# Two-layer decoder trunk on one core: nine seven-product pairs in the last SwiGLU, shared sums added to x before the last blocks, nine low parts finished by transfers out of DRAM

## The chip, the cores and the metric

One core of a Trainium2 chip runs the whole program. The metric is the device time of one execution in microseconds (us), lower is better. The kernel before took 966.36 us (median of three runs, 966.13 to 967.34).

## The reference

A trunk of two layers over 256 rows of width 1024, batch 1, all in float32. Each layer is: half a SwiGLU step, a token mixer, half a SwiGLU step. Every step normalises x, scales and shifts it by vectors worked out from c, and adds its result to x through a gate vector. What the change touches is the last SwiGLU step of the last layer, the end of the program:

```
h = modulate(rms_norm(x, norm_g[1, 2]), sh3, sc3)
x = x + 0.5 * g3[:, None, :] * swiglu(h, w_gate, w_up, w_down)
swiglu(h, w_gate, w_up, w_down) = (silu(h @ w_gate) * (h @ w_up)) @ w_down
```

with h of 256x1024, w_gate and w_up of 1024x2816 and w_down of 2816x1024. The 2816 inner columns are 22 blocks of 128, called f = 0 to 21 here.

## The kernel before

**Three passes.** A float32 product is made of float32r parts: each operand is split in a high part hi (ScalarE rounds it, line 775) and a low part lo = value - hi (VectorE, line 780), and TensorE runs hi*hi, hi*lo and lo*hi (lines 932 to 934, function mm3). For the gate and up blocks the moving operand holds hi and lo of both row halves side by side, 512 columns, so a weight block takes one 512-column pass with its hi (line 1192) and one 256-column pass with its lo (line 1189). Weights stream from DRAM through three buffers called raw (SyncE issues the loads, line 904); hi and lo have eight buffers each.

**Gate and up.** In the last SwiGLU, f = 0 to 3 come first, then two f at a time: a gate tile and an up tile of 1024x256, each split in two halves of 128x1024. For four of the gate tiles (f = 8, 12, 16, 20) the low part of the second half is not subtracted by VectorE: ScalarE writes -1 times the raw value, rounded to float32r, into lo's buffer (line 777), and an adding transfer issued on GpSimd adds raw, read from its SBUF buffer, to it (line 778). The raw buffer is free again when that transfer has landed.

**Down in pairs.** Two inner blocks k and k+1 of w_down, with both row halves and both halves of the 1024 output columns, are a 2x2 by 2x2 product: eight 128x128x512 products of three passes. `pair_step` makes it of seven, after Strassen and Winograd: VectorE forms four sums of the left side (`left_sums`, lines 1113 to 1116) and four of the weights (`seven`, lines 879 to 883). Three of the products go to the sums of single output quarters (mm tiles), four to shared sums p1, p6, p7, p5 (tr tiles) which `seven_down` later combines. EARLY says how many pairs stand behind which gate and up block: before, two each behind the blocks that end at f = 5, 9, 13 and 17, eight pairs, k = 0 to 15. After each group the shared sums are copied out of PSUM into SBUF tiles named kept (line 1268) or added to them (line 1264). The remaining k = 16 to 21 of w_down run plainly by STEPS "2 4": a step of two k and a closing one of four, the tail.

**The end.** The quarters are named (row half, column half). Before, the combined shared sum of quarter (1,1) is multiplied by the gate and added to x early (`base`, lines 1316 and 1317); for the other three it is added to the quarter's PSUM sum at the end (line 1050), then follow gate product, addition to x and the transfer out (lines 1052 to 1056, function `resid`). Quarter (1,1) is finished last, in two column halves; the second is made with weights already multiplied by the gate (line 1374), so that one addition (line 1384) and a transfer out (line 1385) end the program.

**The order.** Nothing runs in the order of the code. `Order` records all instructions, places them with a table of durations and rules, and fixes each engine's order; TRIALS is a list of random shifts (a time and a seed), found beforehand, that are applied one after the other. Where an engine's order says so, an instruction waits behind the one ahead of it.

Of the kernel before, what the change touches and what calls it, by code (L numbers as in the profile page):

```python
# [12 lines left out]
F32 = mybir.dt.float32  # L13
F32R = mybir.dt.float32r
# [3 lines left out]
ALU = mybir.AluOpType  # L18
AX = mybir.AxisListType
PSUM = bass.MemoryType.PSUM  # L20
DRAM = bass.MemoryType.DRAM

P = 128
# [6 lines left out]
FB = 512  # L30
TAIL = 4
B1 = 7
STEPS = {(1, 0): "4 p p 4 4 2 4", (1, 1): "2 4"}
PAIRED = {(1, 0): 12, (1, 1): 0}
EARLY = {(1, 1): {6: 2, 10: 2, 14: 2, 18: 2}}
SLOTS = 10
DMA_AT = [("gate", f) for f in range(8, 22, 4)]
BEFORE = {key: sum(EARLY.get(key, {}).values()) for key in STEPS}
PAIRS = {key: steps.count("p") + BEFORE[key] for key, steps in STEPS.items()}
BY_DMA = [("ffn_w_" + n, (1, 1), f * P) for n, f in DMA_AT]  # L40
# [174 lines left out]
def bcast_row(ap, n, parts=P):  # L215
# [23 lines left out]
MARGIN = 400.0  # L239
ROUND_OF_ORDER = 2  # L240
PORT = 250.0

TRIALS = ((22.03, 5), (28.53, 74), (28.53, 181), (22.87, 220), (27.57, 328), (27.57, 471), (34.83, 1096),
# [18 lines left out]
ENGINES = ("PE", "DVE", "Activation", "Pool", "SP")  # L262


def elements(ap):
    return math.prod(c for _, c in ap.ap[1:])
# [51 lines left out]
class Order:  # L318
# [4 lines left out]
    def __init__(self, nc, tc, rank, held, late, anchor):  # L323
# [14 lines left out]
        n = len(self.ins)  # L338
# [4 lines left out]
        for ks in sums.values():  # L343
# [3 lines left out]
        self.cost = [duration(i, a) for i, a in zip(self.ins, self.aps)]  # L347
        self.mode = [self.pe_mode(i, a) for i, a in zip(self.ins, self.aps)]
        self.two = [type(i).__name__ in ("InstTensorTensor", "InstCustomDveAnt") for i in self.ins]
        self.table = [{"Silu": "s", "Sin": "s", "Exp": "e"}.get(str(getattr(i, "func", "")).rsplit(".", 1)[-1])  # L350
                      if e == "Activation" else None for i, e in zip(self.ins, self.eng)]
        self.succ, self.after = [[] for _ in range(n)], [[] for _ in range(n)]
# [13 lines left out]
        for name, us in self.uses.items():  # L366
            t = self.tiles[name]
# [98 lines left out]
    def place(self, need, until=1e15):  # L466

        n = len(self.ins)
# [7 lines left out]
        in_pool, pool_end = {}, {}  # L476
        for t, r in self.ring.items():
            in_pool[r[0]] = in_pool.get(r[0], 0) + users[t]
        flight, dma_free, mode, table, idle_from, wide, paired = [], FIRST_BYTE, None, None, 0.0, 0, 0.0

        def grant(r):
# [53 lines left out]
        while placed < n:  # L535
# [36 lines left out]
                occ, dur, mode = occ + d, dur + d, now  # L572
            if e == "DVE" and self.two[k]:
                paired = t + occ
            if e == "Pool" and not self.dma[k]:
                at_once = [x for x in avail["DVE"]] + [(need[j], j) for r, j in known["DVE"] if r < t + PORT]
                lock = paired
                if at_once and free["DVE"] < t + PORT and self.two[min(at_once)[1]]:
                    lock = max(free["DVE"], t) + self.cost[min(at_once)[1]][0]
                d = lock - t - 150.0  # L580
                occ, dur = occ + max(d, 0.0), dur + max(d, 0.0)
# [89 lines left out]
def trunk(ctx: ExitStack, tc: tile.TileContext, a: dict, out: bass.AP):  # L671
    nc = tc.nc
# [96 lines left out]
    c_b = cp.tile([P, D], F32, name="c_b")  # L769


    def split(src, n, by_dma=False):
        hi = splitp.tile([P, n], F32R, tag="hi", name=nm("hi"))
        lo = splitp.tile([P, n], F32R, tag="lo", name=nm("lo"))
        nc.scalar.activation(hi, src, AF.Copy)  # L775
        if by_dma:
            nc.scalar.activation(lo, src, AF.Copy, scale=-1.0)
            nc.gpsimd.dma_start(lo.bitcast(F32), src, accum_op=ALU.add)
            return hi, lo
        nc.vector.tensor_tensor(lo, src, hi.bitcast(F32), op=ALU.subtract)  # L780
        return hi, lo
# [111 lines left out]
    def wload():  # L893
# [7 lines left out]
        else:  # L901
            raw = rawp.tile([P, kt * cols], F32, tag="raw", name=nm("raw"))
        n = P * kt * cols
        nc.sync.dma_start(raw, a["w"][wpos[0]:wpos[0] + n].rearrange("(p f) -> p f", p=P))
        wpos[0] += n
        if whole:
            return [raw[:, j * cols:(j + 1) * cols] for j in range(kt)]
# [4 lines left out]
        pairs = []  # L912
        for k0 in range(0, kt, per):
            n = min(per, kt - k0)
            hi, lo = split(raw[:, k0 * cols:(k0 + n) * cols], n * cols, parts[0] in BY_DMA and k0 >= kt // 2)
            for j in range(n):
                pairs.append((hi[:, j * cols:(j + 1) * cols], lo[:, j * cols:(j + 1) * cols]))
        return pairs
# [354 lines left out]
    def seven_down(strassen, gT, sums, after, ada_to):  # L1273
# [40 lines left out]
        def base(t, half, y):  # L1314
            x = xs[t][:, halves[half]]
            nc.vector.tensor_tensor(y, y, gate[:, halves[half]], op=ALU.mult)
            nc.vector.tensor_tensor(x, x, y, op=ALU.add)
# [14 lines left out]
            plus(v[:, lo], p7, u[:, hi])  # L1332
            plus(v[:, hi], p5, u[:, hi])
        if at == (1, 1):
            base(1, 1, p5)
            rest = {(0, 0): p1, (1, 0): p7, (0, 1): p6}
        else:
            base(0, 0, u[:, lo])
            base(0, 1, v[:, hi])
# [23 lines left out]
        wl = nextw()  # L1363
        for t in range(NT):
            rows([t], 0, first_tail, wl, end - 1)
            resid(t, 0, acc[t, 0], gate, True, plus=rest[t, 0])
        wl = nextw()
        rows([0], 1, first_tail, wl, end - 1)
        resid(0, 1, acc[0, 1], gate, True, plus=rest[0, 1])
        more = tr_tile()[:, :256]  # L1370
        scaled = adap.tile([P, TAIL * 256], F32, tag="adaw", name=nm("scaled"))
        cs = slice(768, 1024)
# [7 lines left out]
            mm3(last[:, :256], *gT[first_tail + j, 1], *[x[:, :256] for x in w], start=j == 0 and not begun, stop=j == TAIL - 1)  # L1380
        for j in range(TAIL):
            mm3(more, *gT[first_tail + j, 1], *[x[:, j * 256:(j + 1) * 256] for x in ends], start=j == 0, stop=j == TAIL - 1)
        resid(1, 1, last, gate, True, done=256)
        nc.vector.tensor_tensor(xs[1][:, cs], more, xs[1][:, cs], op=ALU.add)
        nc.scalar.dma_start(out[0, P:, cs], xs[1][:, cs])
        after(1)
# [725 lines left out]
```

## Time and profile before

| what | value |
|---|---|
| median of three runs | 966.36 us |
| span of the profiled execution, first to last instruction | 964.5 us |
| PE (TensorE) busy | 959.0 us, 99% |
| DVE (VectorE) busy | 893.7 us, 93% |
| ACT (ScalarE) busy | 642.7 us, 67% |
| POOL (GpSimd) busy | 76.5 us, 8% |
| HBM read | 258.53 MB |
| last SwiGLU, first to last product | about 782 to 961 us of the span |

The profiled execution has no separate time of its own beside its span of 964.5 us; what a run counts around the span is the difference to the runs' median, 1.9 us. The profile gives each engine's busy time, the chain of work that ended last, groups of instructions with their mean durations, who waited for whom, and a timeline. PE's busy time counts pipelined passes that overlap, so a busy PE says that it had something in flight, not that it issued at its best rate: a 512-column pass shows 0.39 us, but the next one starts 0.23 us after it.

### The profile page before, as it was taken

The numbers are of one execution on the slowest core, as the hardware profiler recorded it, in microseconds if no ns is written. First come the engines' busy times: TensorE is split into PE (matmuls) and PEld (weight loads), VectorE is DVE, ScalarE is ACT, GpSimd is POOL, SyncE is SP. The second block draws the span as 40 slices with busy tenths as digits, with TensorE's granted clock in tenths as the row PEclk, the third lists the DMA queues.
The fourth block names the chain that finished last, engine by engine and source line by source line (L and its number), as shares of the span: only waits on it lengthen the run. The fifth ranks groups of instructions, "written<-read, shape, count | busy, mean of one in ns | idle before, by whom it ended". The sixth has DMA issues, their size and how long they took to land.

```text
span 964.5 us, 15470 instructions
## 1 busy us (share of the span) xinstructions
PE 959.0 (99%) x5519; PEld 824.4 (85%) x5519; DVE 893.7 (93%) x1627; ACT 642.7 (67%) x1220; POOL 76.5 (8%) x112
## 2 busy tenths in 40 slices
PE   9999999999999999999999999999999999999998
PEld 7998888888888888888888888888889888888887
DVE  7999999798999999999779899899999879999997
ACT  5688665477757965565358656663689887776662
POOL 0002100012231100000000000000143100000000
PEclk9999999999999999999999999999999999999999
DMA  9978998889796799989878989659553354865761
GB/s 349 408 284 266 366 323 309 352 313 354 278 331 214 271 361 337 338 321 321 341 291 314 333 327 340 233 204 329 179 184 120 117 197 175 272 230 199 259 211 73
DMA packets 57692, 265.85 MB, mean 276 GB/s; under 512 B 7536, under 2 KB 9360, under 8 KB 39696
## 3 DMA queue, kind: packets, MB, share of 16 engines
q1 hardware_dynamic: 55584, 259.12, 73.3%
q0 software_dynamic: 1408, 5.24, 2.3%
q8 instruction: 43, 0.70, 0.3%
q10 hardware_dynamic: 624, 0.51, 0.2%
q14 instruction: 33, 0.27, 0.1%
HBM read 258.53 MB, written 4.22 MB: 272 GB/s over the span
## 4 chain that ended last, share of the span: by engine, by line
PE 94%; DMA 2%; DVE 2%; ACT 2%; issue 1%; SPq 0%; ACTq 0%; DVEq 0%
PE tr L1192 16%; PE mm L932 14%; PE mm L934 14%; PE mm L933 14%; PE mm L1192 9%; PE tr L1189 9%; PE mm L1189 5%; PE at L1479 1%; PE at L1413 1%; PE at L1449 1%; PE tr L932 1%; PE tr L933 1%; PE tr L934 1%; PE mm L2061 1%; PE tr L985 1%
## 5 line engine op out<-in xcount | busy, mean ns | idle before, releaser
L775 ACT ACTIVATE hi<-raw 128x1024 fp32r<-128x1024 f32 (+3 forms) x306 | 307.7, 1028 | 126.9 <-PE mm L934 59.1
L780 DVE TENSOR_TENSOR lo<-raw,hi 128x1024 fp32r<-128x1024 f32 (+3 forms) x302 | 351.8, 1191 | 31.4 <-ACT hi L775 25.9
L1192 PE MATMUL tr<-h,hi 128*128 128x512 f32 x688 | 164.6, 390 | 0.0
L1192 PEld LDWEIGHTS tr<-h,hi 128*128 128x128 f32 x688 | 127.5, 188 | 25.3
L793 DVE CUSTOM_DVE_ANT_0 adaw<-adaw,c_b,cols 128x1024 f32<-128x1024 f32 x96 | 121.9, 1282 | 0.7 <-DMA adaw<-in_ada_dram 0.7
L932 PE MATMUL mm<-hi,gh 128*128 128x512 f32 (+1 forms) x292 | 113.8, 390 | 0.0
L933 PE MATMUL mm<-lo,gh 128*128 128x512 f32 (+1 forms) x292 | 113.3, 388 | 0.0
L934 PE MATMUL mm<-hi,gl 128*128 128x512 f32 (+1 forms) x292 | 113.3, 388 | 0.0
L1192 PE MATMUL mm<-h,hi 128*128 128x512 f32 x416 | 98.2, 391 | 0.2 <-DVE u L1089 0.2
L934 PE MATMUL mm<-hi,h 128*128 128x512 f32 (+1 forms) x240 | 93.1, 394 | 0.0
L932 PE MATMUL mm<-hi,h 128*128 128x512 f32 (+1 forms) x240 | 92.8, 396 | 0.1
L933 PE MATMUL mm<-lo,h 128*128 128x512 f32 (+1 forms) x240 | 92.7, 393 | 0.0
L1192 PEld LDWEIGHTS mm<-h,hi 128*128 128x128 f32 x416 | 77.0, 188 | 15.7 <-DVE u L1089 0.4
L1189 PEld LDWEIGHTS tr<-h,lo 128*128 128x128 f32 x688 | 87.0, 191 | 2.6
L1189 PE MATMUL tr<-h,lo 128*128 128x256 f32 x688 | 87.9, 283 | 0.0
L934 PEld LDWEIGHTS mm<-hi,gl 128*128 128x128 f32 x292 | 54.8, 188 | 11.2
L933 PEld LDWEIGHTS mm<-lo,gh 128*128 128x128 f32 x292 | 54.9, 188 | 10.7
L932 PEld LDWEIGHTS mm<-hi,gh 128*128 128x128 f32 x292 | 54.9, 188 | 10.6
L831 DVE CUSTOM_DVE_ANT_0 adaw<-adaw,c_b,g_cols 128x1024 f32<-128x1024 f32 x48 | 61.5, 1291 | 0.0
L972 POOL TENSOR_TENSOR rstd<-ssq,mhalf 128x1 f32<-128x1 f32 x12 | 13.4, 1117 | 527.5 <-DVE ssq L967 485.2
L1189 PE MATMUL mm<-h,lo 128*128 128x256 f32 x416 | 54.4, 284 | 0.1
L1189 PEld LDWEIGHTS mm<-h,lo 128*128 128x128 f32 x416 | 52.7, 191 | 1.6 <-DVE lo L780 0.2
(291 smaller groups left out, 1607.8 us busy)
## 6 DMA issues: line engine op xcount, KB each, us to landing
raw<-in_w_dram SPq DMA_DIRECT2D x140, 1024.0 KB, 5.9
adaw<-in_ada_dram SPq DMA_DIRECT2D x155, 512.0 KB, 5.8
raw<-in_w_dram SPq DMA_DIRECT2D x14, 512.0 KB, 4.3
bias_d<-bt SPq DMA_DIRECT2D x12, 256.0 KB, 4.4
gate<-gate_d SPq DMA_DIRECT2D x6, 512.0 KB, 6.5
bg<-bias_d POOLq DMA_DIRECT2D x4, 768.0 KB, 6.3
adaw<-in_ada_dram SPq DMA_DIRECT2D x10, 256.0 KB, 5.7
raw<-in_w_dram SPq DMA_DIRECT2D x4, 576.0 KB, 5.1
```

Source lines behind the costliest of these rows:

```text
L775: nc.scalar.activation(hi, src, AF.Copy)
L780: nc.vector.tensor_tensor(lo, src, hi.bitcast(F32), op=ALU.subtract)
L793: nc.vector.tensor_tensor_reduce(wt, wt, c_b, 1.0, b, op0=ALU.mult, op1=ALU.add, accum_out=m_cols[:, i, c:c + 1])
L831: nc.vector.tensor_tensor_reduce(wt, wt, c_b, 1.0, g[:, k:k + 1], op0=ALU.mult, op1=ALU.add, accum_out=g[:, k:k + 1])
L932: nc.tensor.matmul(ps, lh, rh, start=start, stop=False)
L933: nc.tensor.matmul(ps, lh, rl, start=False, stop=False)
L934: nc.tensor.matmul(ps, ll, rh, start=False, stop=stop)
L972: nc.gpsimd.tensor_tensor(r, stats[t], mhalf[:, 0:1], op=ALU.pow)
L985: nc.tensor.transpose(kslice(pt, j), kslice(y, j), ident)
L1189: nc.tensor.matmul(ps[f][i][:, S:], w, hs[0], start=False, stop=k == KD - 1)
L1192: nc.tensor.matmul(ps[f][i], w, hs[2], start=k == 0, stop=False)
L1413: nc.tensor.matmul(ps3[:, i, :], qTs(e, t), kTs(e, nk), start=True, stop=True)
```

## The change

STEPS of the last SwiGLU becomes "4" and EARLY puts three pairs instead of two behind the block that ends at f = 17: nine pairs, k = 0 to 17, and only the tail of four k runs plainly. DMA_AT now names nine gate tiles (f = 4, 6, ... 20). The adding transfer reads its addend from the weight array in DRAM, not from the raw buffer. All four quarters of the shared sums are multiplied by the gate and added to x by `base`, and `resid` has no extra addition any more; quarter (1,1) has no plain products ahead of the tail, so its last sum starts there and its `resid` is half as wide. The planner learns a rule: a GpSimd AFFINE_SELECT (function grips) and a VectorE instruction on SBUF hold each other up. TRIALS is a new list, so every engine's order is new from the first microseconds on.

```
 B1 = 7
-STEPS = {(1, 0): "4 p p 4 4 2 4", (1, 1): "2 4"}
+STEPS = {(1, 0): "4 p p 4 4 2 4", (1, 1): "4"}
 PAIRED = {(1, 0): 12, (1, 1): 0}
-EARLY = {(1, 1): {6: 2, 10: 2, 14: 2, 18: 2}}
+EARLY = {(1, 1): {6: 2, 10: 2, 14: 2, 18: 3}}
 SLOTS = 10
-DMA_AT = [("gate", f) for f in range(8, 22, 4)]
+DMA_AT = [("gate", f) for f in range(4, 22, 2)]
...
+GRIP = 50.0, 725.0, 577.0, 160.0
...
-TRIALS = ((22.03, 5), (28.53, 74), (28.53, 181), (22.87, 220), (27.57, 328), (27.57, 471), (34.83, 1096),
+TRIALS = ((28.52, 62196), (27.3, 97909), (34.82, 84045), (34.77, 72623), (34.58, 54429), (39.69, 96378), (39.67,
...
+        self.grips = [type(i).__name__ == "InstTensorScalarAffineSelect" for i in self.ins]
+        self.port = [e == "DVE" and all(x.tensor.space not in (PSUM, DRAM) for x in a) and max(elements(x) for x in a) > 8
+                     for e, a in zip(self.eng, self.aps)]
...
-            if e == "Pool" and not self.dma[k]:
+            if e == "DVE" and self.port[k]:
+                d = max(0.0, gripped[1] - t) if t >= gripped[0] else 0.0
+                occ, dur = occ + d, dur + d
+                porting = t + occ
+            if e == "Pool" and self.grips[k]:
...
+                dur = max(GRIP[1], lock - t + GRIP[2])
+                occ = dur - 70.0
+                gripped = since, t + dur - GRIP[3]
+            elif e == "Pool" and not self.dma[k]:
...
-    def split(src, n, by_dma=False):
+    def split(src, n, again=None):
...
-        if by_dma:
+        if again is not None:
             nc.scalar.activation(lo, src, AF.Copy, scale=-1.0)
-            nc.gpsimd.dma_start(lo.bitcast(F32), src, accum_op=ALU.add)
+            nc.gpsimd.dma_start(lo, again.bitcast(F32R), accum_op=ALU.add)
             return hi, lo
...
-            hi, lo = split(raw[:, k0 * cols:(k0 + n) * cols], n * cols, parts[0] in BY_DMA and k0 >= kt // 2)
+            at = slice(k0 * cols, (k0 + n) * cols)
+            hi, lo = split(raw[:, at], n * cols, place[:, at] if parts[0] in BY_DMA and k0 >= kt // 2 else None)
...
         if at == (1, 1):
-            base(1, 1, p5)
-            rest = {(0, 0): p1, (1, 0): p7, (0, 1): p6}
+            for t, half, y in ((0, 0, p1), (1, 0, p7), (0, 1, p6), (1, 1, p5)):
+                base(t, half, y)
...
-            resid(t, 0, acc[t, 0], gate, True, plus=rest[t, 0])
+            resid(t, 0, acc[t, 0], gate, True)
...
-        resid(1, 1, last, gate, True, done=256)
+        if begun:
+            resid(1, 1, last, gate, True, done=256)
+        else:
+            resid(1, 1, last[:, :256], gate, True, part=slice(0, 256))
```

The kernel after is 22 to 25 lines longer from there on: line 780 becomes 800, 777 becomes 797, 1192 becomes 1214, 932 to 934 become 954 to 956.

**Place one: the first transfers.** ScalarE's rows before, where the first adding transfer is prepared (lo_9394, gate tile f = 8; hi_9389 and hi_9393 are the two high halves of its tile; gh is the high part of a gated block; g_9425 is the gate sum of f = 6, copied out of PSUM):

```order
L775 ACTIVATE hi_9389<-raw_9387 128x1024
L775 ACTIVATE hi_9393<-raw_9387 128x1024
L777 ACTIVATE lo_9394<-raw_9387 128x1024
L947 ACTIVATE gh_9234<-g_9226 128x256
L947 ACTIVATE gh_9262<-g_9254 128x256
L775 ACTIVATE hi_9495<-raw_9493 128x1024
L1088 ACTIVATE g_9425<-tr_9367 128x256
```

ScalarE's rows after, where the transfer of the gate tile f = 6 is prepared (lo_9336); the kept rows copy the first group's shared sums out of PSUM:

```order
L795 ACTIVATE hi_9331<-raw_9329 128x1024
L795 ACTIVATE hi_9335<-raw_9329 128x1024
L795 ACTIVATE hi_9373<-raw_9371 128x1024
L797 ACTIVATE lo_9336<-raw_9329 128x1024
L1290 ACTIVATE kept_9352<-tr_9298 128x512
L1290 ACTIVATE kept_9356<-tr_9300 128x512
L1290 ACTIVATE kept_9358<-tr_9301 128x512
```

TensorE's rows after at the same place, from the end of the first two pairs (mm_9325) to the first use of lo_9336 (tr_9369 and tr_9370 are gate and up sums of f = 6 in the banks that the kept copies free):

```order
L956 MATMUL mm_9325<-hi_9294,gl_9170 128x512
L1214 MATMUL tr_9369<-h_8818,hi_9331 128x512 x4
L1214 MATMUL tr_9369<-h_8818,hi_9335 128x512 x4
L1214 MATMUL tr_9370<-h_8818,hi_9373 128x512 x4
L1214 MATMUL tr_9370<-h_8818,hi_9377 128x512 x4
L1211 MATMUL tr_9369<-h_8818,lo_9332 128x256 x4
L1211 MATMUL tr_9369<-h_8818,lo_9336 128x256 x4
```

The preparation of a transfer now stands ahead of the copies that free the banks, and its low part is used in the block that follows at once.

**Place two: the end of the last group of pairs.** TensorE's rows before, the last products of the eighth pair and the first gate passes of f = 18 (tr_10389):

```order
L932 MATMUL mm_9324<-hi_10325,gh_10169 128x512
L933 MATMUL tr_10331<-lo_10326,sums_10178 128x512
L934 MATMUL tr_10331<-hi_10325,sums_10178 128x512
L934 MATMUL tr_10330<-hi_10319,sums_10178 128x512
L933 MATMUL mm_9324<-lo_10326,gh_10169 128x512
L934 MATMUL mm_9324<-hi_10325,gl_10170 128x512
L1192 MATMUL tr_10389<-h_8818,hi_10356 128x512 x4
```

TensorE's rows after, the ninth pair (sums_10315, the left sums of f = 16 and 17) and the first gate passes of f = 18 (tr_10446):

```order
L954 MATMUL tr_10344<-hi_10379,sums_10315 128x512
L954 MATMUL tr_10342<-hi_10379,sums_10315 128x512
L954 MATMUL mm_9309<-hi_10374,sums_10315 128x512
L955 MATMUL mm_9309<-lo_10375,sums_10315 128x512
L954 MATMUL tr_10343<-hi_10385,sums_10315 128x512
L955 MATMUL mm_9302<-lo_10375,gh_10306 128x512
L956 MATMUL mm_9309<-hi_10374,sums_10315 128x512
L1214 MATMUL tr_10446<-h_8818,hi_10412 128x512 x4
L1214 MATMUL tr_10446<-h_8818,hi_10416 128x512 x2
L955 MATMUL tr_10344<-lo_10380,sums_10315 128x512
L956 MATMUL tr_10344<-hi_10379,sums_10315 128x512
```

The last pair uses inner blocks that were computed just ahead of it, and gate passes of the next block stand between its products.

**Place three: the end.** VectorE's last rows before (kept tiles are the shared sums, ry is a scratch tile, mm_9301, mm_9324 and mm_9308 the sums of quarters (0,0), (1,0) and (0,1), mm_10647 and tr_10718 the two halves of (1,1)):

```order
L1050 TENSOR_TENSOR kept_9350<-mm_9301,kept_9350 128x512
L1052 TENSOR_TENSOR ry_10679<-kept_9350,gate_9904 128x512
L1053 TENSOR_TENSOR x_94<-x_94,ry_10679 128x512
L1050 TENSOR_TENSOR kept_9356<-mm_9324,kept_9356 128x512
L1052 TENSOR_TENSOR ry_10696<-kept_9356,gate_9904 128x512
L1053 TENSOR_TENSOR x_95<-x_95,ry_10696 128x512
L1050 TENSOR_TENSOR kept_9354<-mm_9308,kept_9354 128x512
L1052 TENSOR_TENSOR ry_10713<-kept_9354,gate_9904 128x512
L1053 TENSOR_TENSOR x_94<-x_94,ry_10713 128x512
L1052 TENSOR_TENSOR ry_10749<-mm_10647,gate_9904 128x512
L1053 TENSOR_TENSOR x_95<-x_95,ry_10749 128x512
L1384 TENSOR_TENSOR x_95<-tr_10718,x_95 128x256
```

VectorE's last rows after (mm_9302, mm_9325, mm_9309, mm_10748 and tr_10741 are the same sums):

```order
L1074 TENSOR_TENSOR ry_10705<-mm_9302,gate_9907 128x512
L1338 TENSOR_TENSOR kept_9354<-kept_9354,gate_9907 128x512
L1075 TENSOR_TENSOR x_94<-x_94,ry_10705 128x512
L1339 TENSOR_TENSOR x_95<-x_95,kept_9354 128x512
L1074 TENSOR_TENSOR ry_10721<-mm_9325,gate_9907 128x512
L1075 TENSOR_TENSOR x_95<-x_95,ry_10721 128x512
L1074 TENSOR_TENSOR ry_10737<-mm_9309,gate_9907 128x512
L1075 TENSOR_TENSOR x_94<-x_94,ry_10737 128x512
L1074 TENSOR_TENSOR ry_10773<-mm_10748,gate_9907 128x256
L1075 TENSOR_TENSOR x_95<-x_95,ry_10773 128x256
L1409 TENSOR_TENSOR x_95<-tr_10741,x_95 128x256
```

The three additions of kept are gone from the end; one quarter's `base` stands among the closing rows, the other three stand ahead of the tail's last low parts.

More of the change, by code (lines that the diff above doesn't have):

```diff
@@ L478, in place @@
             in_pool[r[0]] = in_pool.get(r[0], 0) + users[t]
+        gripped, porting = (0.0, 0.0), 0.0
         flight, dma_free, mode, table, idle_from, wide, paired = [], FIRST_BYTE, None, None, 0.0, 0, 0.0
@@ L574, in place @@
                 paired = t + occ
-            if e == "Pool" and not self.dma[k]:
+            if e == "DVE" and self.port[k]:
[3 more added lines that the diff above has]
+            if e == "Pool" and self.grips[k]:
+                soon = [x[:2] for x in avail["DVE"]] + [(need[j], j) for r, j in known["DVE"] if r < t + GRIP[0]]
+                lock = since = max(porting, t)
+                if soon and free["DVE"] < t + GRIP[0] and self.port[min(soon)[1]]:
+                    lock = max(free["DVE"], t) + self.cost[min(soon)[1]][0]
+                    since = lock - 20.0
+                dur = max(GRIP[1], lock - t + GRIP[2])
+                occ = dur - 70.0
+                gripped = since, t + dur - GRIP[3]
+            elif e == "Pool" and not self.dma[k]:
                 at_once = [x for x in avail["DVE"]] + [(need[j], j) for r, j in known["DVE"] if r < t + PORT]
@@ L903, in wload @@
         n = P * kt * cols
-        nc.sync.dma_start(raw, a["w"][wpos[0]:wpos[0] + n].rearrange("(p f) -> p f", p=P))
+        place = a["w"][wpos[0]:wpos[0] + n].rearrange("(p f) -> p f", p=P)
+        nc.sync.dma_start(raw, place)
         wpos[0] += n
@@ L1365, in seven_down @@
             rows([t], 0, first_tail, wl, end - 1)
-            resid(t, 0, acc[t, 0], gate, True, plus=rest[t, 0])
+            resid(t, 0, acc[t, 0], gate, True)
         wl = nextw()
         rows([0], 1, first_tail, wl, end - 1)
-        resid(0, 1, acc[0, 1], gate, True, plus=rest[0, 1])
+        resid(0, 1, acc[0, 1], gate, True)
         more = tr_tile()[:, :256]
```

38 rows, old and new, of the table TRIALS are left out of this document.

## The prediction

> **What bounds the kernel now.** I read the page's busy times and its chain first, then the stretches, then the timeline where TensorE shows a gap.
>
> ```profile
> span 964.5 us, 15470 instructions
> PE 959.0 (99%) x5519; PEld 824.4 (85%) x5519; DVE 893.7 (93%) x1627; ACT 642.7 (67%) x1220; POOL 76.5 (8%) x112
> PE 94%; DMA 2%; DVE 2%; ACT 2%; issue 1%; SPq 0%; ACTq 0%; DVEq 0%
> ```
>
> TensorE is busy all the time and carries 94% of the chain that ended last. So a pass taken away is time gained where it stood, and work on another engine costs only where it makes TensorE wait. The stretches say where waiting is left (columns: stretch, its length, then busy time and count of PE, PEld, DVE, ACT, POOL, granted clock, DMA share, GB/s):
>
> ```profile
> 0.00:40.00 40.00, 38.31 (x266) 33.75 (x267) 31.90 (x63) 24.22 (x50) 2.36 (x24) 1.00 0.99 371
> 40.00:120.00 80.00, 79.61 (x729) 72.18 (x728) 77.04 (x161) 62.12 (x129) 10.91 (x42) 1.00 0.86 317
> ...
> 320.00:680.00 360.00, 360.00 (x1879) 309.15 (x1878) 335.69 (x520) 215.29 (x372) 4.31 (x3) 1.00 0.85 313
> 680.00:800.00 120.00, 119.93 (x718) 103.52 (x717) 109.23 (x287) 103.61 (x259) 28.29 (x24) 1.00 0.43 148
> 800.00:960.00 160.00, 160.00 (x851) 138.39 (x850) 155.03 (x248) 105.08 (x164) 3.50 (x4) 1.00 0.61 211
> ```
>
> TensorE idles 1.7 us in the first 40, 0.4 in the next 80, and nothing in the last 160 us, where the named parts of the change lie. There VectorE is the neighbour to watch: 155 of 160 us. The end, from the timeline:
>
> ```profile
> 960.48 0.69 DVE L1053 TENSOR_TENSOR x<-x,ry 128x512 f32<-128x512 f32 x1
> ...
> 960.87 0.28 PE L934 MATMUL tr<-hi,gl 128*128 128x256 f32 x1
> 961.27 0.42 DVE L1384 TENSOR_TENSOR x<-tr,x 128x256 f32<-128x256 f32 x1
> 961.73 0.35 ACTq L1385 DMA_DIRECT2D out_dram<-x  x1
> ```
>
> The last addition waits for the last pass, not for VectorE, which came free at 961.17. What follows 960.87 is the same in both kernels: 3.6 us.
>
> **The products.** Passes of 512 and of 256 columns follow each other like this, products first (914.31 to 917.26, thirteen steps in all), then a block's sixteen lo passes and the row behind them:
>
> ```profile
> 914.31 0.39 PE L932 MATMUL mm<-hi,sums 128*128 128x512 f32 x1
> ...
> 917.26 0.39 PE L932 MATMUL mm<-hi,gh 128*128 128x512 f32 x1
> ```
>
> ```profile
> 894.07 2.08 PE L1189 MATMUL tr<-h,lo 128*128 128x256 f32 x16
> 895.98 3.82 PE L1192 MATMUL tr<-h,hi 128*128 128x512 f32 x16
> ```
>
> That is 2.95 / 13 = 0.227 us and 1.91 / 16 = 0.119 us. Step "2" was 2 x 2 x 2 = 8 products, 24 passes; the ninth pair has 7 products, 21 passes. Three passes fewer: **-0.68 us**, all of it on the path, since TensorE has no gap in this stretch. Every other pass remains.
>
> **VectorE and ScalarE in the last SwiGLU.** The prices are in the groups of that stretch (mean ns of one behind the comma):
>
> ```profile
> L780 DVE TENSOR_TENSOR lo<-raw,hi 128x1024 fp32r<-128x1024 f32 x48 | 58.1, 1234 | 2.1 <-ACT hi L775 2.0
> L780 DVE TENSOR_TENSOR lo<-t,hi 128x1024 fp32r<-128x1024 f32 x16 | 19.0, 1233 | 0.0
> L831 DVE CUSTOM_DVE_ANT_0 adaw<-adaw,c_b,g_cols 128x1024 f32<-128x1024 f32 x8 | 10.2, 1286 | 0.0
> L879 DVE TENSOR_TENSOR t<-raw 128x1024 f32<-128x1024 f32 x8 | 9.8, 1230 | 0.0
> L882 DVE TENSOR_TENSOR t<-t,raw 128x512 f32<-128x512 f32 x8 | 5.6, 699 | 0.0
> L1113 DVE TENSOR_TENSOR s<-g,g 128x128 f32<-128x128 f32 x6 | 1.8, 298 | 0.0
> L1050 DVE TENSOR_TENSOR kept<-mm,kept 128x512 f32<-128x512 f32 x3 | 2.1, 692 | 1.1 <-PE mm L934 1.1
> L777 ACT ACTIVATE lo<-raw 128x1024 fp32r<-128x1024 f32 x4 | 4.2, 1047 | 0.0
> L947 ACT ACTIVATE sums<-s 128x512 fp32r<-128x512 f32 x8 | 5.0, 622 | 0.0
> ```
>
> VectorE loses five subtractions for the five new transfers (6.2 us), two for step "2" (2.5), and three additions at the end (2.1): 10.8. It gains a pair: t13 1.23, two half rows of t24 1.4, low parts of 512 once (0.7, as L882) and of 1024 three times (3.7), four left sums (1.2) and their low part (0.7): 8.9; and three more `base`, six rows of 0.69: 4.1. Net +2.2 us on 155 of 160, so it fits, with little over. ScalarE gets about five copies of 1.05 and some of the pair's, 7 to 8 us on 105 of 160: covered. The cover of both is TensorE's gate and up passes, 22 us for two blocks.
>
> The tight spot is the ninth pair, whose left sums come from f = 16 and 17, the blocks just ahead of it. Between the last pass of f = 17 and the first product with sums_10315 stand 40 passes, 9.1 us. In that time VectorE's order has three subtractions or sums of 1.23, three rows of 0.70, two of 256 columns (0.42 as L1384) and four of 0.30 up to the last left sum: 7.8 us; ScalarE's high part (0.62) makes 8.4. It is on time by 0.7 us; the low parts behind it (2.4 us of VectorE) are needed 0.7 to 3.4 us later. If VectorE is on time as before, the cost is 0; if each row takes its full duration with no overlap, about 1 us. I take **+0.2 us**.
>
> **The end.** From the last pass of quarter (0,0) to the last pass of all stand 17 of 512 and 21 of 256 columns: 3.9 + 2.5 = 6.4 us. VectorE has eight rows of 0.69 and two of 0.42 in it: 6.4 us by durations, less as they overlap (0.1 us was free before). Bounds 0 to +0.3; I take **0**. Before, quarter (1,1) had rows of 512 there; they are half as wide now.
>
> **The transfers.** The page of issues gives sizes and the median from issue to landing; then comes the first transfer on GpSimd, with VectorE beside it:
>
> ```profile
> raw<-in_w_dram SPq DMA_DIRECT2D x14, 512.0 KB, 4.3
> raw<-in_first_dram SPq DMA_DIRECT2D x4, 512.0 KB, 9.3
> lo<-raw POOLq DMA_DIRECT2D x4, 512.0 KB, 5.5
> ```
>
> ```profile
> 828.84 1.29 DVE L831 CUSTOM_DVE_ANT_0 adaw<-adaw,c_b,g_cols 128x1024 f32<-128x1024 f32 x1
> 829.23 0.96 POOL L778 DMA_DIRECT2D lo<-raw  x1 [39.91 <-ACT gh L947]
> ```
>
> VectorE's row beside GpSimd's issue keeps its 1.29 us (mean 1.286), so five more issues cost it nothing. No adding transfer out of DRAM is in the trace: the plain load of that size lands in 4.3 us, in the crowded first microseconds in 9.3; I take 5.5, the adding one. GpSimd and its queue have nothing else to do in this stage. At place one, ScalarE prepares lo_9336 ahead of the kept copies. Sixteen passes of 512 and four of 256 lie between the bank's first use and lo_9336's: 4.1 us; and if ScalarE copies p1 as soon as it is done (18 passes earlier, 4.1 us), there are 8.2 us from preparation to use, against 0.9 + 5.5 = 6.4. So 0 if ScalarE is prompt, up to 6.4 - 4.7 = 1.7 us if it is as late as the order allows (4.1 and the copy of 0.6). TensorE waited for none of the four before; I take 0. What goes is a wait of SyncE for the raw buffers:
>
> ```profile
> SPq L904 <- DMA lo<-raw: 18.1, 3, 6.8
> ```
>
> Loads then start earlier; as TensorE waits for no load in this stretch, that gains nothing.
>
> **The new order.** Everything outside the last SwiGLU does the same work in another order. What can be lost or won there is TensorE's idle time. One gap has a cause that the new planner rule knows:
>
> ```profile
> 84.41 1.05 POOL L1587 TENSOR_SCALAR_AFFINE_SELECT bt<-bt 128x512 f32<-128x512 f32 x1 [4.98 <-ACT bt L1585]
> ...
> 84.80 1.73 DVE L831 CUSTOM_DVE_ANT_0 adaw<-adaw,c_b,g_cols 128x1024 f32<-128x1024 f32 x1
> ...
> 88.69 0.36 PE L1189 MATMUL mm<-h,lo 128*128 128x256 f32 x1
> ...
> 89.26 0.96 PE L1192 MATMUL mm<-h,hi 128*128 128x512 f32 x3 [0.21 <-DVE u L1089]
> ```
>
> VectorE's row beside AFFINE_SELECT took 1.73 instead of 1.29 us, the rows behind it came late, and TensorE's next pass began 0.57 us after a 256-column pass instead of 0.12: 0.45 us lost. [...] A planner that knows it can put other work there. Bounds: 1.1 us gained (the 2.1 of the first 120 us less about 1.0 before the first pass), or as much lost by a worse order, for nothing in the order alone says that a wait is gone. I take **-0.5 us**, the row's 0.45.
>
> Sum: -0.68 + 0.2 + 0 + 0 - 0.5 = -1.0 us; span 964.5 becomes 963.5. The median is 1.9 above the span: 966.36 - 1.0 = **965.4 us**.
>
> **The rivals.** *The order pays more.* All 1.1 us of early idle go and the ninth pair costs nothing, and small gaps before 800 us close up too, like this one at the stage's first products:
>
> ```profile
> 781.53 0.82 PE L985 MATMUL tr<-ident,y 128*128 128x128 f32 x6
> 782.42 0.50 PE L932 MATMUL mm<-hi,h 128*128 128x512 f32 x1
> 782.76 0.39 PE L933 MATMUL mm<-lo,h 128*128 128x512 f32 x1
> ```
>
> The transposes end at 782.35, the product starts 0.07 later and its successor 0.34 after it instead of 0.227: 0.2 us. Three such make -0.68 - 1.1 - 0.6 = -2.4, 964.0 us. For it: every engine's order is new, and the rule on AFFINE_SELECT is right. Against: the old order had been searched too. 0.30.
>
> *The gain is eaten at the ninth pair.* VectorE's rows run at full durations, TensorE waits 1 us there, and the new order gives nothing: -0.68 + 1.0 = +0.3, 966.7 us. For: the 0.7 us above is all the room. Against: no wait at all in this stretch before. 0.08.
>
> *The transfers out of DRAM come late (slower).* A landing of 9.3 instead of 5.5 makes 10.2 from preparation, against 8.2 at lo_9336: 2.0 us there, and about 0.5 at each of the eight others, whose low parts also stand behind a few passes of their own block: +6.0 - 1.0 = +5.0, 971.4 us. It decides from a landing of 7.3 us on if ScalarE is prompt. Against: DMA was 0.99 busy where 9.3 was seen, 0.61 here. [...] 0.07.
>
> **How the numbers follow.** The forecast has 0.55, and its own range is 964.2 to 966.4 by the bounds above. The range takes in the better part of the first rival and leaves out the third: 963.4 to 967.0. Faster or slower counts from 0.2%, 1.9 us, about what a measurement of this kernel can tell from no change: faster 0.33 (the first rival and 0.03 of the forecast's low end), slower 0.07, same 0.60.
>
> **What would show it.** Right: PE x5516 against x5519; no PE wait for lo at line 1211; the last addition 0.4 us behind the last pass; AFFINE_SELECT without a gap in PE behind it. Wrong: PE waiting for a landing or for sums in the last SwiGLU, landings of 8 us and more, or a change of PE's time before 780 us of over 1.5 us.

## The result, and the profile after it

The changed kernel takes 974.64 us (median of 6 runs, 974.12 to 980.64) beside 966.39 for the kernel before (6 runs, 966.13 to 968.41): ratio 1.0094, 95% interval 1.0081 to 1.0108. It is 8.25 us slower, where 1.0 us faster was forecast, and lies beyond the range given. Busy times and chain of the changed kernel (TensorE has the 5516 passes forecast, but DMA now holds 6% of the chain):

```profile
span 973.0 us, 15478 instructions
PE 962.4 (99%) x5516; PEld 823.6 (85%) x5516; DVE 895.7 (92%) x1635; ACT 646.0 (66%) x1228; POOL 75.8 (8%) x117
PE 87%; DMA 6%; issue 3%; DVE 2%; ACT 2%; POOL 0%; SPq 0%; ACTq 0%; POOLq 0%; DVEq 0%
```

The page's share of PE is 99% in both and hides the loss. The stretches of the changed kernel show where it is (the columns are those of the prediction):

```profile
40.00:120.00 80.00, 80.00 (x736) 73.02 (x735) 74.76 (x160) 63.83 (x128) 11.67 (x42) 1.00 0.83 308
...
800.00:960.00 160.00, 154.97 (x806) 131.93 (x805) 149.14 (x244) 110.11 (x173) 7.79 (x9) 0.99 0.68 224
```

TensorE idles 5.0 us in the last 160, where it idled nothing before. Milestones say the same: the first product of the last SwiGLU begins at 782.85 us (782.42 before) and the last pass at 969.32 (960.87), so 186.47 - 178.45 = 8.0 us are lost in the last SwiGLU. The 0.4 us ahead of it say little: with the kernel before's own order this product begins at 784.52 in before_dram, below. The two largest of TensorE's waits in the whole program (total, number, longest), and the transfers that it waits for (issues: count, size, median landing):

```profile
PE tr L1211 <- DMA lo<-in_w_dram: 5.0, 4, 3.2
PE tr L1977 <- DVE zeros L1935: 1.0, 1, 1.0
```

```profile
lo<-in_w_dram POOLq DMA_DIRECT2D x9, 512.0 KB, 9.2
```

The landings are 8.0 to 10.5 us, the median 9.2 instead of the 5.5 that was taken. The third of the four waits for lo is the longest; this is TensorE's timeline around it, and the stretches around the fall of the granted clock:

```profile
897.78 0.28 PE L1211 MATMUL tr<-h,lo 128*128 128x256 f32 x1
901.30 2.08 PE L1211 MATMUL tr<-h,lo 128*128 128x256 f32 x12 [3.25 <-DMA lo<-in_w_dram]
903.18 2.76 PE L1214 MATMUL tr<-h,hi 128*128 128x512 f32 x6
```

```profile
898.96:902.38 3.42, 1.08 (x9) 1.08 (x10) 0.25 (x2) 0.24 (x1) 0.00 (x0) 1.00 1.02 386
902.38:905.79 3.41, 3.41 (x13) 2.83 (x12) 2.98 (x8) 2.52 (x5) 0.00 (x0) 0.50 1.03 299
905.79:909.20 3.41, 3.41 (x24) 3.15 (x23) 3.41 (x5) 1.59 (x5) 0.00 (x0) 1.00 0.23 43
```

Behind a wait of 3.25 us the clock is 0.50 for 3.41 us, which costs about 3.41 x 0.50 = 1.7 us more. Then it is 1.00 again. In the 3.42 us ahead of the fall TensorE was busy for 1.08.

**Why a landing is late.** SyncE's and GpSimd's issues of the changed kernel around the second transfer, with ScalarE's row that both wait for:

```profile
823.10 1.04 ACT L797 ACTIVATE lo<-raw 128x1024 fp32r<-128x1024 f32 x1
...
824.17 6.67 SPq L925 DMA_DIRECT2D raw<-in_w_dram  x3
...
824.45 0.86 POOL L798 DMA_DIRECT2D lo<-in_w_dram  x1 [23.14 <-ACT lo L797]
```

ScalarE's copy ends at 824.14. With a DRAM source it is the last reader of the raw buffer, so it lets two things go at once: the next 1 MB load into that buffer, issued 0.03 us later, and the transfer, issued 0.31 us later. What the DMA engines then move, in the 4 us from the transfer's issue (queue, packets, MB, share; q1 are the loads, q0 the transfer) and in the 4 us behind those:

```profile
DMA packets 122, 0.91 MB, mean 228 GB/s; under 512 B 9, under 2 KB 9, under 8 KB 14
...
q1 hardware_dynamic: 121, 0.90, 82.4%
q8 instruction: 1, 0.02, 1.5%
```

```profile
q0 software_dynamic: 144, 0.52, 68.0%
q1 hardware_dynamic: 78, 0.51, 34.8%
```

In the first window there is no packet of the transfer at all; in the second there are all 144. The transfer's packets come behind those of the load that its own buffer has let go; it lands 8.0 us after its issue, and TensorE, which is there sooner, waits:

```profile
832.49 1.70 PE L1211 MATMUL tr<-h,lo 128*128 128x256 f32 x12 [0.86 <-DMA lo<-in_w_dram]
```

### The profile page after: what moved, and what is told of

It reads as the page before. It is cut to its first block, busy times and chain, and to the rows that moved or that the text cites. A ratio compares the mean times of both kernels' runs of the same rounds, so it can differ in the third digit from the quotient of the medians.

```text
span 973.0 us, 15478 instructions
## 1 busy us (share of the span) xinstructions
PE 962.4 (99%) x5516; PEld 823.6 (85%) x5516; DVE 895.7 (92%) x1635; ACT 646.0 (66%) x1228; POOL 75.8 (8%) x117
## 4 chain that ended last, share of the span: by engine, by line
PE 87%; DMA 6%; issue 3%; DVE 2%; ACT 2%; POOL 0%; SPq 0%; ACTq 0%; POOLq 0%; DVEq 0%
PE tr L1214 14%; PE mm L954 12%; PE mm L956 12%; PE mm L955 12%; PE mm L1214 10%; PE tr L1211 8%; PE mm L1211 5%; DMA lo<-in_w_dram 4%; DMA adaw<-in_ada_dram 2%; PE mm L2086 2%; PE at L1504 1%; PE at L1438 1%; PE at L1474 1%; PE tr L2086 1%; PE tr L1606 1%
## 5 line engine op out<-in xcount | busy, mean ns | idle before, releaser
L800 DVE TENSOR_TENSOR lo<-raw,hi 128x1024 fp32r<-128x1024 f32 (+3 forms) x297 | 345.7, 1188 | 27.9 <-ACT hi L795 23.4
L1214 PE MATMUL tr<-h,hi 128*128 128x512 f32 x688 | 168.5, 393 | 0.0
L955 PE MATMUL mm<-lo,gh 128*128 128x512 f32 (+1 forms) x286 | 110.1, 389 | 0.0
L954 PE MATMUL mm<-hi,gh 128*128 128x512 f32 (+1 forms) x286 | 109.9, 389 | 0.0
L956 PE MATMUL mm<-hi,gl 128*128 128x512 f32 (+1 forms) x286 | 109.7, 389 | 0.0
L1211 PE MATMUL tr<-h,lo 128*128 128x256 f32 x688 | 93.3, 284 | 5.0 <-DMA lo<-in_w_dram 5.0
L1211 PEld LDWEIGHTS tr<-h,lo 128*128 128x128 f32 x688 | 89.8, 192 | 9.7 <-DMA lo<-in_w_dram 6.2
L954 PEld LDWEIGHTS mm<-hi,gh 128*128 128x128 f32 x286 | 53.8, 188 | 10.6
```

Source lines behind the costliest of these rows:

```text
L954: nc.tensor.matmul(ps, lh, rh, start=start, stop=False)
L955: nc.tensor.matmul(ps, lh, rl, start=False, stop=False)
L956: nc.tensor.matmul(ps, ll, rh, start=False, stop=stop)
L1211: nc.tensor.matmul(ps[f][i][:, S:], w, hs[0], start=False, stop=k == KD - 1)
L1214: nc.tensor.matmul(ps[f][i], w, hs[2], start=k == 0, stop=False)
```

## The experiments

Twelve kernels ran beside the kernel before, whose median was 966.49 in the first four, then 966.61, 966.64 and 966.58 us. The first four were meant to tell apart the source in DRAM (S), its float32r view (T), nine transfers instead of four (N) and the new order (O).

**sbuf_f32, sbuf_f32r**: the changed kernel's order on every engine, but the transfers read the raw buffer again, as float32 or by float32r names.

```
-nc.gpsimd.dma_start(lo, again.bitcast(F32R), accum_op=ALU.add)
+nc.gpsimd.dma_start(lo.bitcast(F32), src, accum_op=ALU.add)
```

> The changed kernel, every engine's order kept row for row, but the nine adding transfers read their addend from the raw buffer in SBUF with float32 views, as before the change. Theory S (an adding transfer whose source is DRAM lands later) and theory T (the float32r view makes it land later): landings fall from a median of 9.2 to about 5.5 us, TensorE's waits for lo (3.4, 1.0, 0.8 and 0.5 us) go, and with them the stretch of slow passes behind the longest wait (1.5 us): about 974.6 - 7.2 = 967.4 us. Theory N (nine transfers crowd each other, whatever their source): landings stay near 9 us and the time near 974.6. Theory O (the new order is worse by itself): the time stays over 972 with landings at 5.5.

> As the run before it, but source and destination of the transfers are named float32r, as in the changed kernel; the source is the raw buffer in SBUF. Theory S: landings of about 5.5 us and about 967.4 us, as with float32. Theory T: landings of about 9 us and about 974.6 us. Theory N: as theory T here.

Measured: 973.35 us (972.82 to 977.38; ratio 1.0081, 1.0060 to 1.0102) and 972.67 (972.07 to 974.85; 1.0069, 1.0054 to 1.0084). The waits and issues of the first:

```profile
lo<-raw POOLq DMA_DIRECT2D x9, 512.0 KB, 5.4
```

```profile
SPq L929 <- DMA lo<-raw: 71.4, 9, 14.2
```

```profile
PE tr L1218 <- ACT hi L799: 1.1, 1, 1.1
PE tr L958 <- DVE g L1115: 1.0, 2, 0.7
PE tr L959 <- DVE lo L804: 0.9, 2, 0.6
```

```profile
945.98 1.06 ACT L799 ACTIVATE hi<-raw 128x1024 fp32r<-128x1024 f32 x1 [1.53 <-DMA raw<-in_w_dram]
947.09 1.21 PE L1218 MATMUL tr<-h,hi 128*128 128x512 f32 x4 [1.10 <-ACT hi L799]
```

The median landing is short again and TensorE waits for no transfer, yet the time hardly falls. SyncE now waits 71.4 us for buffers that the transfers hold, and TensorE waits in the last SwiGLU for ScalarE's and VectorE's rows. The last two rows show it for the longest of these waits: a load is late, so ScalarE is, and then TensorE; for the others no row here shows it. So T falls: with float32r names the median landing is 5.0 us. S is right on the median landing and wrong on the time: the order was made for buffers that come free early, and TensorE loses on late loads much of what it wins on the transfers. Two of the nine landings are long even so, 9.3 and 9.2 us, with the source in SBUF; load_behind comes back to them.

**before_dram**: the kernel before in its own order, its four transfers read DRAM.

> The kernel before, every engine's order kept, with its four adding transfers reading their addend from DRAM as the changed kernel does. From issue to first use there are 12.9, 9.0, 8.4 and 12.1 us. Theories S and T: landings of about 9 us, so TensorE waits at most about 0.8 us at one or two of the four places: 966.4 to 968 us. Theory N: landings stay at 5.5 and the time at 966.4.

Measured: 966.62 us (965.94 to 968.42; ratio 1.0001, 0.9991 to 1.0010), landings 7.3 in the median instead of 5.5, and no wait of TensorE for them: those four stand 8.4 to 12.9 us ahead of their use. The source alone costs nothing where there is room. The four land in 6.5, 8.0, 5.1 and 8.1 us: the second had a load issued 0.17 us ahead of it, the third none for 3.5 us before and 5.5 us after its issue.

**late_known**: the changed kernel, but the planner takes each transfer to land 3.7 us later; its list of trials is the old one.

> The changed kernel with a planner that knows that these transfers land 3.7 us later; the list of shifts is the same, so the order is new and not searched for. Theory S or T: no wait of TensorE for lo over 0.5 us is left, and the time lies below 974.6 by what the unsearched order does not cost again: 967 to 972 us. Theory O: still 973 or more.

Measured: 976.49 us (976.35 to 978.12; ratio 1.0108, 1.0093 to 1.0123). The waits went elsewhere:

```profile
PE tr L960 <- DVE gl L974: 2.2, 1, 2.2
PE tr L1215 <- DMA lo<-in_w_dram: 1.4, 1, 1.4
```

This run is inconclusive on the transfers, since an order whose trials were found for other delays may be worse by itself. Next to be tested was the reading of the section above, called theory L (in line): a transfer is late because of a load that goes first. S now stands for a read out of DRAM that is late by itself.

**load_behind**: every order as in the changed kernel; behind each transfer GpSimd reads a column of the raw buffer, so that the buffer comes free after the transfer's issue.

```
 nc.gpsimd.dma_start(lo, again.bitcast(F32R), accum_op=ALU.add)
+nc.gpsimd.tensor_tensor(seen, src[:, :1], mhalf[:, 0:1], op=ALU.mult)
```

> The changed kernel with every engine's order as it was; behind each of the nine adding transfers GpSimd reads one column of the raw buffer, so the load that this buffer lets go is issued behind the transfer and not 0.28 us ahead of it. Theory L (in line): a transfer comes late because that load's 1 MB stands ahead of it on the DMA engines, about 3 us. It expects first packets 1.4 to 2.0 us after the issue instead of 4.3 to 4.9, a median landing of 4.5 to 6, no wait of TensorE for lo, and the time less 5.7 (gaps), 1.5 (low clock) and some of 1.7 (smaller waits): 966 to 968. Theory S (a read out of DRAM is late by itself): landings stay at 8 to 9, 973 to 975. Theory O (the new order is worse whatever the transfers do): landings fall, the time stays over 970.

Measured: 968.51 us (967.67 to 970.03; ratio 1.0018, 1.0010 to 1.0027). Issues around the same transfer, the DMA queues in the 4 us from its issue, the landings of all nine, and all of TensorE's waits:

```profile
826.82 0.88 POOL L801 DMA_DIRECT2D lo<-in_w_dram  x1 [22.16 <-ACT lo L800]
...
827.44 0.61 POOL L803 TENSOR_TENSOR seen<-raw,mhalf 128x1 f32<-128x1 f32 x1
...
828.07 6.69 SPq L931 DMA_DIRECT2D raw<-in_w_dram  x3
```

```profile
q0 software_dynamic: 111, 0.45, 64.7%
q1 hardware_dynamic: 16, 0.04, 2.6%
```

```profile
lo<-in_w_dram POOLq DMA_DIRECT2D x9, 512.0 KB, 5.7
```

```profile
PE tr L1983 <- DVE zeros L1941: 1.0, 1, 1.0
PE mm L2092 <- ACT whi L2071: 0.3, 1, 0.3
PE tr L1013 <- ACT y L1008: 0.2, 1, 0.2
```

With the load 1.25 us behind the transfer and not 0.28 ahead, 111 of its 144 packets go in the window that held none, and no wait for lo is left. Of 8.25 us over the kernel before, 1.90 are left; the last SwiGLU takes 179.0 us (785.21 to 964.21) instead of 186.47. L is shown in so far as a load that goes first makes the transfer late: the source is the same and S falls, and there are still nine transfers, so N falls. But for the first, the transfers stand in pairs, 3.6 to 6.3 us apart. The first of each pair and the one that stands alone land in 5.1 to 5.7 us; the second of a pair takes 10.0 to 10.6, behind loads that were issued ahead of it, and has the room. In the changed kernel, all four waits for lo are for the first of a pair.

The two late landings of sbuf_f32 show the other side: a source in SBUF, and late all the same behind two loads that were issued 1.7 and 1.3 us ahead. SyncE's issues and GpSimd's, then the landing:

```profile
830.23 11.98 SPq L929 DMA_DIRECT2D raw<-in_w_dram  x4
...
831.93 0.85 POOL L802 DMA_DIRECT2D lo<-raw  x1 [5.46 <-ACT lo L801]
...
lo<-raw POOLq DMA_DIRECT2D x1, 512.0 KB, 9.3
```

The order of the issues alone does not decide. In the changed kernel one load was issued 0.24 us behind a transfer, and even so the 4 us from the transfer's issue hold packets of the loads alone:

```profile
936.08 0.86 POOL L798 DMA_DIRECT2D lo<-in_w_dram  x1 [38.15 <-ACT lo L797]
...
936.32 0.33 SPq L925 DMA_DIRECT2D raw<-in_w_dram  x1
...
q1 hardware_dynamic: 95, 0.77, 65.8%
```

At 856.18, with a load issued 0.20 us behind, 16 of the transfer's 144 packets went in that time.

**quarter**: every order as in the changed kernel, the loads where they stood, a quarter of each transfer; the kernel leaves out the addition for the other three quarters of these low parts.

```
+nc.gpsimd.dma_start(lo[:, :256], again[:, :256].bitcast(F32R), accum_op=ALU.add)
```

> The changed kernel with every engine's order as it was, but each adding transfer moves a quarter of its columns (three quarters of these low parts stay -raw, so part of the computation is left out). The loads stand where they stood. L and S both expect the first packet as late as before, 4.3 to 4.9 us, but a landing of about 6 to 7 (a quarter of 2.8 us of packets), so that nearly all waits of TensorE for lo go: 966.5 to 969. O expects over 970. If the time stays at 974, the transfers' lateness is not what costs.

Measured: 967.65 us (966.98 to 968.74; ratio 1.0010, 1.0001 to 1.0018), landings 6.1 in the median, no wait for lo, 178.94 us for the last SwiGLU. Two ways to an earlier landing give the same end: lateness is what cost, not the order (O falls for the last SwiGLU).

**line_known**: the changed kernel's operations; the planner lets SyncE's issues of the next 0.7 us stand ahead of a transfer, and its trials were found with that.

```
+b = BEHIND if x == "Pool" and self.dma[min(avail[x])[1] if avail[x] else known[x][0][1]] else 0.0
+if s + b < t:
+    t, e, back = s + b, x, b
```

> The changed kernel, the same operations, but the planner lets SyncE's issues of the next 0.7 us go ahead of a GpSimd transfer on the DMA engines, and its list of trials was searched with that. L expects that the order can then hide what stays late: landings of 7 to 9 us, each far enough ahead of its use, no wait of TensorE for lo over 0.5 us, 964.5 to 967. S expects the same landings, and no better than 970 where the planner counts only the load as delay. O: over 970.

Measured: 969.79 us (7 runs, 967.14 to 972.28; ratio 1.0029, 1.0015 to 1.0044), landings 9.4 in the median, one wait for lo:

```profile
PE tr L1221 <- DMA lo<-in_w_dram: 1.1, 1, 1.1
```

It missed the 964.5 to 967 expected, but takes 4.9 us off by the order alone: with landings as late as before, the waits for lo fall from 5.0 to 1.1 us. That late landings cost nothing where the order knows of them is not shown; this order's last SwiGLU still takes 181.4 us.

**nine_sbuf4**: nine pairs and the early sums, with the kernel before's four transfers out of the raw buffer; trials found for it.

> Nine pairs and the shared sums added early, as in the changed kernel, but with the kernel before's four transfers out of the raw buffer; VectorE makes the five other low parts (6.2 us). Order searched for this kernel. If the nine pairs cost nothing by themselves and only the nine transfers do, 966 to 968. If the ninth pair's VectorE work is what the transfers had to pay for, TensorE waits for DVE rows in the last SwiGLU: 968 to 972. Transfers land in 4.5 to 6.5 us.

Measured: 970.75 us (970.47 to 972.94; ratio 1.0046, 1.0035 to 1.0058). TensorE's wait at the last pairs, with VectorE's and ScalarE's rows ahead of it:

```profile
924.18 0.70 DVE L908 TENSOR_TENSOR t<-raw,t 128x512 f32<-128x512 f32 x1
```

```profile
925.00 1.06 ACT L800 ACTIVATE hi<-t 128x1024 fp32r<-128x1024 f32 x1 [1.22 <-DVE t L908]
```

```profile
926.11 0.50 PE L959 MATMUL mm<-hi,gh 128*128 128x512 f32 x1 [1.29 <-ACT hi L800]
```

VectorE is busy without a break there, its t comes late, ScalarE waits 1.22 us for it and TensorE 1.29 for ScalarE. So with VectorE making five more low parts, TensorE does wait for the ninth pair's sums. The kernel is 4.1 us slower than the one before, 3.7 of them in the last SwiGLU (182.1 us); TensorE's waits there make 1.6, and what the rest is wasn't resolved. Another order may do better.

**front_after, front_before, front_before2, front_after2** ask what the new order ahead of the last SwiGLU costs, by exchanging it between the kernels (front_before and front_before2 are load_behind with the old order in front):

```
+order = self.work_out()[1]
+for e, text in FRONT.items():
...
+    order[e] = [next(was) if k < 6984 else k for k in order[e]]
```

> The kernel before, operation for operation; only the instructions ahead of the last SwiGLU stand on each engine in the order that the changed kernel gives them. Theory F: that new order costs by itself what is left of the loss once the transfers are on time. By TensorE's idle time in the traces it wins 1.0 us between 40 and 120 us and loses 1.1 between 120 and 280, up to 0.7 between 320 and 680 and about 1.5 between 680 and 800, so 1.6 to 2.3 us over the kernel before: 968.0 to 969.0. Rival: the rest of the loss lies in the last SwiGLU's own work, and the front is a wash or the small gain that was forecast: 965.9 to 966.8.

> The kernel with the loads issued behind the transfers, and the kernel before's order ahead of the last SwiGLU. F expects 968.5 less 1.6 to 2.3: 966.2 to 966.9, that is nine pairs and nine transfers then cost what they save, with small waits of 1.6 us in the last SwiGLU against 0.68 of passes. Rival: no change from 968.5.

> The same as the one before it, but the last SwiGLU's order is a searched one. If the small waits of the last SwiGLU (1.6 us) come from the order and not from the work, it gains part of them: 965.3 to 966.5, a version as fast as the kernel before or a little faster. If they come from the work, as the one before it.

Measured: 972.86 us (970.41 to 974.08; ratio 1.0064, 1.0052 to 1.0077), 968.72 (968.29 to 970.19; 1.0023, 1.0014 to 1.0032) and 969.93 (968.83 to 971.53; 1.0036, 1.0024 to 1.0049). The first is spoilt by the exchange itself, as a row at the seam and the clock behind it (0.50 for 6.83 us) show:

```profile
795.78 0.47 PE L1202 MATMUL tr<-ident,y 128*128 128x128 f32 x1 [3.33 <-ACT y L1197]
```

```profile
794.52:801.35 6.83, 5.57 (x14) 4.45 (x15) 1.01 (x2) 2.73 (x8) 0.00 (x0) 0.50 0.00 0
```

The second missed 966.2 to 966.9: with the old order in front, the first product begins at 782.32 us, as early as in the kernel before, but the last SwiGLU takes 180.58, and nothing is won. The third was not faster either. So the last run exchanges only up to places where both orders have done the same instructions:

> The kernel before, operation for operation, with the changed kernel's order ahead of the last SwiGLU; each engine's order is exchanged up to a place at which both orders have done the same instructions, so that no instruction is late at the seam. Theory F (the new order costs by itself): 968.0 to 969.0. Rival, by the first product of the last SwiGLU, which begins at 782.42 us in the kernel before and at 782.85 in the changed kernel: the order is a wash, 966.3 to 967.2. The forecast's term for it, -0.5, would give 966.1.

Measured: 968.14 us (967.77 to 969.49; ratio 1.0017, 1.0008 to 1.0026). A wait at the seam is left here too:

```profile
791.83 0.50 PE L1146 MATMUL mm<-hi,h 128*128 128x512 f32 x1 [0.64 <-ACT h L1161]
```

The gap around it is 0.80 us, and the last SwiGLU takes 179.40 instead of 178.45. So of the 1.56 us lost, 0.95 lie behind the seam. The other 0.6 can't be put on the order in front, for the traces of one order differ by more. Much of that arises ahead of TensorE's first product with a loaded weight. It begins at 11.04 us in the changed kernel and at 13.45 in load_behind, where the clock is halved just then (the last line):

```profile
11.04 1.89 PE L2078 MATMUL mm<-z,raw 128*128 128x256 f32 x8
```

```profile
13.45 1.73 PE L2084 MATMUL mm<-z,raw 128*128 128x256 f32 x7
...
10.15:13.56 3.41, 3.41 (x13) 2.16 (x12) 2.15 (x6) 1.92 (x4) 0.00 (x0) 0.50 1.03 393
```

From that product to the first one of the last SwiGLU, the new order takes 771.8 us in the changed kernel, 771.8 in load_behind, 771.3 in quarter, 771.2 in front_after and 772.1 here; the old one takes 771.4 in the kernel before and in front_before, 771.5 in front_before2 and 772.8 in before_dram. As far as these traces can tell, that is the rival, a wash; the 0.5 us that was to be won shows in none of them.

## Why the prediction was wrong

The step that failed is in "The transfers": "No adding transfer out of DRAM is in the trace: ... I take 5.5, the adding one", and with it "TensorE waited for none of the four before; I take 0". The landing was 9.2, and by the prediction's own reckoning the wait decides from 7.3. So the term "The transfers", put at 0, measured 7.5 us. The slower rival had the late landing (9.3), TensorE's wait for it and 971.4 us, and got 0.07; it didn't have what makes the landing late. The prediction took DMA's busy share over the stretch, 0.61, as evidence against it; but the share that counts is that of the microseconds behind the issue, and there a load that the same event releases fills 82.4%.

The sentence that should have warned stands just behind: "Loads then start earlier; as TensorE waits for no load in this stretch, that gains nothing." It asked who gains from the earlier load and not who then stands behind it. The wait of SyncE that went away (18.1 us for three buffers) was what kept the buffer's own load out of the transfer's way: with the wait back, in sbuf_f32, the median landing is 5.4 again.

Point by point:

- Products, -0.68: right in the count (5516). The saving can't be seen alone; with the transfers on time the last SwiGLU still takes 179.0 against 178.45 us.
- VectorE and the ninth pair, +0.2: no wait of TensorE for sums in the changed kernel, and in load_behind the largest step between two passes behind 800 us is 0.50 instead of 0.23, at 925.47. VectorE's busy time rose by 2.0 us, where 2.2 was worked out. Right, but with nine transfers: with four (nine_sbuf4), TensorE waits 1.6 us at the last pairs.
- The end, 0: right. The last addition starts 0.32 us behind the last pass:

```profile
969.32 0.28 PE L956 MATMUL tr<-hi,gl 128*128 128x256 f32 x1
969.64 0.42 DVE L1409 TENSOR_TENSOR x<-tr,x 128x256 f32<-128x256 f32 x1
```

- The transfers, 0: wrong. 7.5 us of the last SwiGLU (186.47 - 179.0): 5.0 in four waits and about 1.7 in the low clock behind the longest; the other 0.8 wasn't resolved. The room that was worked out, at lo_9336, was right: TensorE came there 7.2 us behind the issue (7.3 reckoned), and 8.0 - 7.2 is about the wait of 0.86. At the other eight places no room was worked out. At the sixth TensorE came 6.8 us behind the issue and the landing took 10.0; the rival's 0.5 for each of these places was far too little there (3.25), and the low clock was in no term.
- The new order, -0.5: not there. TensorE's 0.39 us of idle between 40 and 120 us are gone (80.00 busy of 80), as was said of the rule on AFFINE_SELECT. But up to the last SwiGLU nothing is won: 771.8 us from the first product with a loaded weight, against 771.4 before. Whether the new order loses anything isn't shown, since the old one takes 771.4 to 772.8.

What is still open: the 1.0 to 1.9 us by which quarter and load_behind stay above the kernel before. The last SwiGLU makes 0.5 of it in both. The rest, 0.5 and 1.4, lies ahead of it, where traces of one order differ by as much, and wasn't resolved. No version of nine pairs was found that beats the kernel before.

## What to carry to other kernels

Where an edit frees a buffer earlier, ask what is issued the moment it comes free, and what else waits for the same event: a large load released together with a small, urgent transfer went first here, whether it was issued 0.28 us ahead or 0.24 us behind. Take the busy share of a resource from the microseconds in which the new work stands, not from the stage. An order that a planner has packed tightly leaves no room for a delay that its costs don't hold: transfers out of DRAM cost nothing where they had 8.4 us of room and more (before_dram, four of them), and 7.5 us where four of nine lacked it.

## What the runs showed of the hardware

- SyncE issued its load 0.03 us after the event that both waited for, GpSimd its transfer 0.31 us after it. With the load 0.28 us ahead, or in one place 0.24 us behind, no packet of the transfer was seen for 4 us behind its issue; with the load 1.25 us behind, 111 of 144 were. In the first of these cases 121 of the 122 packets of these 4 us were the loads'. Whether the transfer stood in its queue and waited, or came to its queue late, these runs don't tell apart.
- With next to nothing in the way, an adding transfer of 512 KB landed in 4.5 us out of SBUF (sbuf_f32) and in 5.1 to 5.2 us out of DRAM (load_behind); behind loads it took up to 9.3 us out of SBUF (sbuf_f32) and up to 10.6 out of DRAM (load_behind).
- Behind a wait of 3.25 us TensorE's granted clock was 0.50 for 3.41 us; behind one of 1.29 us (nine_sbuf4) it stayed at 1.00. In late_known, behind a wait of 0.8 and, four passes later, one of 2.2 us, it was 0.50 for 6.83 us (928.84 to 935.67). In the 3.4 us ahead of these two falls TensorE was busy for 1.08 and 1.47 us; in the 3.41 us around the wait of 1.29 us it was busy for 2.10.
- In the kernel before, an AFFINE_SELECT of 128x512 took 0.72 us at 92.10, beside VectorE's rows that read PSUM, and 1.80 us at 101.66, beside a subtraction of 128x1024 between SBUF tiles that began 0.01 us later. VectorE's row at 84.80 took 1.73 us beside one, where the mean is 1.29. In the changed kernel they took 0.72 to 1.80 us, and TensorE has no idle time between 40 and 120 us.
